# Weight buffers, staging tiles, score banks and the end of layer A regrouped in a two-layer attention trunk

## The chip, the cores and the metric

One core of one Trainium2 chip runs the whole program. The metric is device time in microseconds of one execution, the median of three runs. An execution that is profiled gives, besides its time, a span (first to last instruction) and the instructions of each engine.

## What is computed

A trunk of two layers over 528 positions (16 learned meta tokens, then 512 frames), 1024 wide, in float32, and a last norm; the meta rows are dropped from the output. Attention is block-causal: a query sees keys of its own chunk of 64 frames and of earlier ones; the 16 meta tokens are a chunk of their own that everybody sees.

```python
# layer A: differential attention, 8 heads of 2 x 64, values of 128
q, k, v = split(rms_norm(h) @ w_qkv); q, k = rotary(q), rotary(k)
a = softmax(q1 @ k1.T) - lam * softmax(q2 @ k2.T)
h = h + (rms_norm(a @ v) * (1 - lam_init)) @ w_o
h = h + (silu(conv3(rms_norm(h) @ w_a)) * (rms_norm(h) @ w_b)) @ w_out      # 2816 wide
# layer B: latent attention, 16 heads, keys of 64 + 32 rotary, values of 64
c_q = rms_norm(rms_norm(h) @ w_dq); q = c_q @ w_uq
c_kv, k_rope = split(rms_norm(h) @ w_dkv); k, v = split(rms_norm(c_kv) @ w_ukv)
h = h + softmax(q @ [k, k_rope].T) @ v @ w_o
h = h + conv_ffn(h)
out = rms_norm(h)[16:]
```

## The kernel before, in words

**Layout.** Activations lie transposed: 128 partitions of features, positions along the free dimension, in 8 feature tiles. Every float32 operand of a large product is split into a high part (a cast to the fast float32 format) and a low part (the difference), and a product is three: high x high, low x high, high x low (`mm3`, L163 to L166).

**Weights.** `wload` (L120) fetches weights over SP's queue into a raw tile (`rawtile`, L117: 1024 columns, 2 slots), and `wsplit` (L104) makes pairs of 512 columns: ScalarE casts the high part (L109), VectorE, or GpSimd while the attention runs, subtracts for the low part (L110). There are 6 slots for pairs (`WBUF`). An output tile of 8 input tiles of 128 columns takes two pairs. The second product of a feed-forward block in layer A has 22 input tiles, so 6 pairs for one output tile. `wload2` fetches two neighbouring output tiles at once, 256 columns. In the last product of the kernel (L1357) the weights are the moving side, a row of 128 inputs is two pairs, and the last `NL` = 3 rows are held together while the four query tiles are finished one after the other.

**Attention scores.** `scores` (L380) makes, for one head and one of its softmaxes, four query tiles that see 144, 272, 400 and 528 keys. It is cut into three steps, s0, s1 and s2. s0 makes the 144 and the 528, the latter as 256 and 272 in two separate banks; s1 the 400 and, beside them, the scores of the 16 meta queries, which it takes from a product with all 128 query columns; s2 the 272. For each, VectorE masks a corner (L393) and reduces to the negative maximum (L394), and ScalarE does the exponential and its row sum (L397). The two halves of the 528 have two maxima, two exponentials and two sums, which L410 and L428 join. All four tiles rotate through `NS` = 3 PSUM banks; two more (psD) serve the projections and three (psT) the transposes and values.

**The order** of each engine's instructions is worked out when the program is built: a planner goes through the program with its own cost estimates and starts on each engine what is ready, earlier statements first (and those under `soon` earlier than they stand). On the chip each engine then runs its list in that order and waits by semaphores. SP issues nearly all DMAs from one queue. So a later statement fills TensorE's holes where its operands are there.

**The end of layer A.** For each of 8 heads: projection of the next head (`qkproj`), scores, `vproj`, the two softmaxes joined (L600), transposes, values, and later `finish_a`, which norms finished heads and writes them as `oh`, `ol`. The root of the norm is done on GpSimd (`soft`), so that ScalarE's table for the exponential stays loaded; for the last head it is ScalarE's square root, which needs another table. To have that loaded early, a dummy square root (L588) reads one sum of the last score set. The meta rows have their own small attention (`meta_soft_a`, `meta_a`); those of the last 8 - KA = 3 heads come at the very end. `out_proj` is two products: heads 0 to KA - 1 (KA = 5) for all 8 output tiles, which can run as filler while later heads are not finished, then heads KA to 7 added to it. In each, one output tile is two halves of 264 positions, and each half adds up its input tiles in one bank of psD.

**Layer B** runs 16 heads in the same manner. `to_heads` (L1022) takes a projected pair of heads from PSUM, splits it into a staging tile `st` (2 slots) and sends the two heads to their own tiles by two DMAs (L1029), since they must change partitions; the queues for weights and for these transfers are the same one. The planner's filler here is a list with due times (`add`, `fill`).

## Time and profile before

| | |
|---|---|
| median of three runs | 1312.9 us (1310.15 to 1313.72) |
| the profiled execution's own time | 1312.65 us |
| its span | 1310.8 us |
| TensorE marked busy | 1279.3 us, 98% of the span |
| VectorE, ScalarE, GpSimd busy | 62%, 47%, 16% |
| mean granted TensorE clock | 0.992 |

Layer A's attention takes the first 300 us, its feed-forward block runs to 690, layer B's latents and attention to about 937, and the second feed-forward block and the final norm to the end. TensorE's matmuls are pipelined and their ends are modelled, so the start of one to the start of the next is the better measure of what one costs. In a row of the timeline the bracket at the end says how long the engine had been idle before it and what ended that.

### The profile page before, as it was taken

The numbers are of one execution on the slowest core, as the hardware profiler recorded it, in microseconds if no ns is written. First come the engines' busy times: TensorE is split into PE (matmuls) and PEld (weight loads), VectorE is DVE, ScalarE is ACT, GpSimd is POOL, SyncE is SP. The second block draws the span as 40 slices with busy tenths as digits, with TensorE's granted clock in tenths as the row PEclk, the third lists the DMA queues.
The fourth block names the chain that finished last, engine by engine and source line by source line (L and its number), as shares of the span: only waits on it lengthen the run. The fifth ranks groups of instructions, "written<-read, shape, count | busy, mean of one in ns | idle before, by whom it ended". The sixth has DMA issues, their size and how long they took to land.

```text
span 1310.8 us, 23833 instructions
## 1 busy us (share of the span) xinstructions
PE 1279.3 (98%) x9412; PEld 1212.6 (93%) x9412; DVE 814.4 (62%) x1702; ACT 619.9 (47%) x1319; POOL 206.1 (16%) x249
## 2 busy tenths in 40 slices
PE   9999999989999999999999899999999999999997
PEld 9899989989999999999999889999899999998886
DVE  6768887667666666533345778885866666662224
ACT  6666566555333433322234677874543333342223
POOL 5333541120000000000021644432200000000000
PEclk9999999989999999999999999999999999999999
DMA  6211211123233332333333545412332333332222
GB/s 211 82 54 56 71 53 49 57 73 100 82 97 90 88 97 82 92 89 90 89 109 62 120 101 122 116 43 81 98 96 87 92 97 97 96 100 92 87 93 81
DMA packets 166000, 117.13 MB, mean 89 GB/s; under 512 B 21248, under 2 KB 154688, under 8 KB 165888
## 3 DMA queue, kind: packets, MB, share of 16 engines
q1 hardware_dynamic: 165888, 115.61, 30.9%
q8 instruction: 74, 1.21, 0.4%
q14 instruction: 38, 0.31, 0.1%
HBM read 102.21 MB, written 2.10 MB: 80 GB/s over the span
## 4 chain that ended last, share of the span: by engine, by line
PE 76%; DVE 3%; ACT 2%; DMA 2%; POOL 1%; issue 1%; SPq 0%; ACTq 0%; POOLq 0%; DVEq 0%
PE psd L166 58%; PE psd L1357 9%; PE b L389 2%; PE ovb L1124 1%; PE tp L1091 1%; PE psd L1061 1%; DVE wlo L110 1%; DMA kt<-st 1%; PE ov L630 1%; DMA q<-st 0%; DVE nm L394 0%; PE tpm L1113 0%; ACT e L397 0%; ACT whi L109 0%; DVE xl L277 0%
## 5 line engine op out<-in xcount | busy, mean ns | idle before, releaser
L166 PE MATMUL psd<-xh,whi 128*128 128x264 f32 (+3 forms) x1664 | 494.2, 297 | 3.1 <-DVE qk L524 2.1
L166 PE MATMUL psd<-xh,wlo 128*128 128x264 f32 (+3 forms) x1664 | 493.1, 296 | 0.0
L166 PE MATMUL psd<-xl,whi 128*128 128x264 f32 (+3 forms) x1664 | 492.2, 296 | 0.7 <-DVE xl L349 0.5
L109 ACT CAST whi<-raw 128x512 fp32r<-128x512 f32 (+2 forms) x346 | 199.7, 589 | 378.7 <-PE psd L166 341.4
L166 PEld LDWEIGHTS psd<-xh,whi 128*128 128x128 f32 x1664 | 313.5, 189 | 12.3 <-DVE qk L524 2.8
L166 PEld LDWEIGHTS psd<-xl,whi 128*128 128x128 f32 x1664 | 313.5, 188 | 9.7 <-DVE xl L349 0.9
L166 PEld LDWEIGHTS psd<-xh,wlo 128*128 128x128 f32 x1664 | 313.4, 188 | 8.2 <-issue 0.4
L110 DVE TENSOR_TENSOR wlo<-raw,whi 128x512 fp32r<-128x512 f32 (+1 forms) x265 | 180.4, 686 | 129.2 <-ACT whi L109 128.0
L110 POOL TENSOR_TENSOR wlo<-raw,whi 128x512 fp32r<-128x512 f32 (+2 forms) x81 | 101.2, 1262 | 135.1 <-ACT whi L109 127.6
L166 PE MATMUL psd<-gh,whi 128*128 128x264 f32 x352 | 100.1, 285 | 0.0
L166 PE MATMUL psd<-gl,whi 128*128 128x264 f32 x352 | 99.9, 284 | 0.0
L166 PE MATMUL psd<-gh,wlo 128*128 128x264 f32 x352 | 99.8, 283 | 0.0
L397 ACT ACTIVATE e<-b,nm 128x272 f32<-128x272 f32 (+3 forms) x160 | 76.5, 481 | 33.5 <-DVE nm L394 19.2
L103 DVE TENSOR_TENSOR wlo<-raw,whi 128x512 fp32r<-128x512 f32 x44 | 28.7, 689 | 86.2 <-ACT whi L102 86.2
L131 POOL TENSOR_TENSOR raw<-raw,smalls 128x1024 f32<-128x1024 f32 x5 | 10.1, 2012 | 384.3 <-DVE acc L251 369.2
L260 DVE TENSOR_TENSOR hT<-psd,hT 128x264 f32<-128x264 f32 (+1 forms) x80 | 33.6, 424 | 57.7 <-PE psd L166 57.6
L102 ACT CAST whi<-raw 128x512 fp32r<-128x512 f32 x44 | 25.4, 619 | 92.7 <-PE psd L1357 75.9
L166 PEld LDWEIGHTS psd<-gl,whi 128*128 128x128 f32 x352 | 66.3, 188 | 0.0
L166 PEld LDWEIGHTS psd<-gh,wlo 128*128 128x128 f32 x352 | 66.3, 188 | 0.0
L166 PEld LDWEIGHTS psd<-gh,whi 128*128 128x128 f32 x352 | 66.2, 188 | 0.0
L394 DVE TENSOR_REDUCE nm<-b 128x1 f32<-128x272 f32 (+3 forms) x160 | 63.7, 423 | 1.2
L761 DVE TENSOR_TENSOR apad<-psd,rt 128x264 f32<-128x264 f32 (+1 forms) x88 | 37.5, 429 | 41.6 <-PE psd L166 41.6
(340 smaller groups left out, 2385.5 us busy)
## 6 DMA issues: line engine op xcount, KB each, us to landing
raw<-in_ffn_w_in SPq DMA_DIRECT2D x88, 512.0 KB
raw<-in_ffn_w_out SPq DMA_DIRECT2D x38, 512.0 KB
raw<-in_w_qkv SPq DMA_DIRECT2D x21, 512.0 KB
q<-st SPq DMA_DIRECT2D x28, 132.0 KB
kt<-st SPq DMA_DIRECT2D x28, 132.0 KB
raw<-in_ffn_w_out SPq DMA_DIRECT2D x8, 384.0 KB
hT<-in_h SPq DMA_DIRECT2D x8, 264.0 KB
q<-y SPq DMA_DIRECT2D x32, 66.0 KB
```

The source lines that it names most:

```text
L102: act.copy(hi, src)
L103: dve.tensor_tensor(lo, src, hi, ALU.subtract)
L109: act.copy(hi, src)
L110: wlo_engine[0].tensor_tensor(lo, src, hi, ALU.subtract)
L166: pe.matmul(ps[:rows, :n], a, xx[:, t0:t0 + n], start=first and ci == 0, stop=last and ci == 2)
L260: dve.tensor_tensor(hT[:, m, a:a + w], ps[:, :w], hT[:, m, a:a + w], ALU.add)
L389: pe.matmul(ps, q[:, q0:q0 + P], k[:, k0:k0 + n], start=i == 0, stop=i == len(parts) - 1)
L394: dve.tensor_reduce(nm[:, c:c + 1], ps, AX.X, ALU.max, negate=True)
L397: act.activation(e[:, o:o + ps.shape[1]], ps, AF.Exp, bias=nm[:, j:j + 1], accum_out=su[:, c:c + 1])
L630: pe.matmul(ov[:, j, :], ts[j][:, b * P:(b + 1) * P], vs[:, b, :], start=b == 0, stop=False)
L761: dve.tensor_tensor(a[:, off:off + n], ps[:, :n], rt[:, t0:t0 + n], ALU.mult)
L1357: pe.matmul(pso[t][n], a, ws[n][b], start=k == 0 and ci == 0, stop=k == NF - 1 and ci == 2)
```

## The change

Raw tiles go from 2 to 3 slots and split pairs from 6 to 5. A score set's 528 query tile is put into one tile of two neighbouring PSUM banks, of which there is one, reduced once and exponentiated once; the other two tiles of a set share one bank. The product for the meta scores loads 16 query columns in place of 128. Layer A's first out-projection part takes six heads, and the late meta rows are those of two heads, done ahead of the last head's transposes; the dummy square root stands behind the meta softmax and reads all four sums. Staging tiles in layer B go from 2 to 3 slots and lie in another pool.

```diff
-KA = KB = 5
+KA, KB = 6, 5
-WT, WBUF, LEAD = 512, 6, 2
+WT, WBUF, RBUF, LEAD = 512, 5, 3, 2
...
-        return wp.tile([P, 1024], F32, tag="raw", name="raw", bufs=2)[:, :n]
+        return wp.tile([P, 1024], F32, tag="raw", name="raw", bufs=RBUF)[:, :n]
...
-    first_ps = [[takeD() for _ in range(2)], [psS.tile([P, 512], F32, tag="s", name="psk") for _ in range(2)]]
+    psk = psS.tile([P, 1024], F32, tag="s2", name="psk", bufs=1)
+    first_ps = [[takeD() for _ in range(2)], [psk[:, i * 512:(i + 1) * 512] for i in range(2)]]
...
-        def qk(ps, q0, k0, n):
+        def qk(ps, q0, k0, n, nq=P):
             for i, (q, k) in enumerate(parts):
-                pe.matmul(ps, q[:, q0:q0 + P], k[:, k0:k0 + n], start=i == 0, stop=i == len(parts) - 1)
+                pe.matmul(ps, q[:, q0:q0 + nq], k[:, k0:k0 + n], start=i == 0, stop=i == len(parts) - 1)
...
-        bank = lambda n: psS.tile([P, 512], F32, tag="s", name=n)
+        bank = lambda n: psS.tile([P, 512], F32, tag="s", name=n, bufs=NS - 2)
 
         def s0():
-            b0 = bank("b0")
+
+            b0 = psS.tile([P, 1024], F32, tag="s2", name="b0", bufs=1)
             qk(b0[:, 0:256], 16, 0, 256)
             qk(b0[:, 256:512], 400, 0, 256)
+            qk(b0[:, 512:784], 400, 256, 272)
             negmax(b0[:, 0:144], 0, 80)
-            negmax(b0[:, 256:512], 3)
-            b1 = bank("b1")
-            qk(b1[:, 0:272], 400, 256, 272)
-            negmax(b1[:, 0:272], 4, 208)
-            dve.tensor_tensor(nm[:, 3:4], nm[:, 3:4], nm[:, 4:5], ALU.min)
+            negmax(b0[:, 256:784], 3, 464)
             ex(b0[:, 0:144], J0[0], 0, 0)
-            ex(b0[:, 256:512], J0[3], 3, 3)
-            ex(b1[:, 0:272], J0[3] + 256, 3, 4)
+            ex(b0[:, 256:784], J0[3], 3, 3)
...
-            qk(b2[:, 400:416], 0, 0, NM)
+            qk(b2[:NM, 400:416], 0, 0, NM, NM)
...
-            dve.tensor_tensor(su[:, 3:4], su[:, 3:4], su[:, 4:5], ALU.add)
...
         if h == HA - 1:
-
-            act.activation(s1a[:, 0, 0:1], es[1][1][:, 3:4], AF.Sqrt)
             ms = meta_soft_a(KA, 8 - KA)
+
+            act.activation(s1a[:, 0, :], es[1][1][:, 0:4], AF.Sqrt)
...
             dve.scalar_tensor_tensor(e1[:, sl], e2[:, sl], cc[:, j:j + 1], e1[:, sl], ALU.mult, ALU.add)
+        if h == HA - 1:
+
+            meta_a(KA, 8 - KA, *ms, soft=False)
...
         osb_s[h] = osb
-        if h == HA - 1:
-            meta_a(KA, 8 - KA, *ms, soft=False)
...
         if h == 5:
-            finish_a(4, KA)
+            finish_a(4, 5)
             meta_a(4, KA - 4, *meta_soft_a(4, KA - 4))
         if h == 6:
-            finish_a(KA, 7)
+            finish_a(5, 7)
...
-            st = ab0.tile([P, 2, HL], F32R, tag="st", name="st", bufs=2)
+            st = ab.tile([P, 2, HL], F32R, tag="st", name="st", bufs=3)
```

The one other line gives a PSUM tile of the first norm the same slot count as the score bank.

## Rows read from the trace of the kernel before

**Rows 1.** The page, busy time by engine.
```profile
PE 1279.3 (98%) x9412; PEld 1212.6 (93%) x9412; DVE 814.4 (62%) x1702; ACT 619.9 (47%) x1319; POOL 206.1 (16%) x249
```
**Rows 2.** The chain that ended last: start, us, what.
```profile
303.60 387.03 PE psd L166 x3185
```
**Rows 3.** Windows: length, busy PE, PEld, DVE, ACT, POOL, granted clock, DMA share, GB/s.
```profile
60.00:70.00 10.00, 9.75 (x68) 9.48 (x69) 5.32 (x23) 5.46 (x17) 0.52 (x1) 0.83 0.16 54
...
270.00:280.00 10.00, 8.47 (x50) 8.21 (x51) 4.72 (x11) 3.36 (x7) 0.00 (x0) 0.69 0.18 52
...
330.00:340.00 10.00, 10.00 (x84) 10.00 (x84) 6.00 (x11) 3.45 (x6) 0.00 (x0) 1.00 0.36 106
...
780.00:790.00 10.00, 8.37 (x61) 8.06 (x60) 8.40 (x23) 7.84 (x24) 6.88 (x9) 0.91 0.58 145
790.00:800.00 10.00, 9.93 (x71) 9.25 (x71) 6.80 (x21) 7.05 (x21) 4.37 (x6) 0.91 0.57 123
```
**Rows 4.** Timeline of layer A's end: ScalarE's table loads, then VectorE, then TensorE.
```profile
243.34 1.28 ACT L588 ACT_TABLE_LOAD   x1
...
245.34 1.28 ACT L397 ACT_TABLE_LOAD   x1
...
267.71 1.28 ACT L645 ACT_TABLE_LOAD   x1
...
243.08 0.73 DVE L670 SCALAR_TENSOR_TENSOR ol<-po,gsub,oh 128x512 fp32r<-128x512 f32 x1
...
247.86 0.69 DVE L110 TENSOR_TENSOR wlo<-raw,whi 128x512 fp32r<-128x512 f32 x1 [2.08 <-ACT whi L109]
...
250.38 0.39 PE L166 MATMUL psd<-oh,whi 128*128 128x264 f32 x1 [2.13 <-DVE hT L260]
...
271.28 0.50 PE L465 MATMUL psv<-ident,om 16*128 16x16 f32 x3 [3.75 <-DVE om L703]
```
**Rows 5.** Groups by form, TensorE, 221 to 243.8 us.
```profile
L166 PE MATMUL psd<-oh,whi 128*128 128x264 f32 x39 | 11.3, 290 | 0.0
```
**Rows 6.** Timeline of TensorE: short products in layer A, in layer B, with 16-column weights.
```profile
38.18 0.17 PE L389 MATMUL b<-ks,qs 128*128 128x16 f32 x1
...
38.52 0.28 PE L166 MATMUL psd<-xl,whi 128*128 128x264 f32 x1
...
743.79 1.05 PE L389 MATMUL b<-kt,q 96*128 96x400 f32 x6
...
744.90 0.28 PE L1061 MATMUL psd<-whi,ckl 128*128 128x256 f32 x1
...
833.23 1.06 PE L458 MATMUL psd<-vms,emT 16*16 16x64 f32 x16
```
**Rows 7.** Waits of ScalarE, 715 to 880 us: us in total, times, longest.
```profile
ACT st L102 <- DMA q<-st: 4.4, 7, 1.0
```
**Rows 8.** Waits of TensorE, 715 to 880 us, the same columns.
```profile
PE psd L166 <- DVE st L103: 1.6, 1, 1.6
PE b L389 <- DMA kt<-st: 1.4, 1, 1.4
```
**Rows 9.** Groups by form, whole run, VectorE and ScalarE: scores.
```profile
L410 DVE TENSOR_TENSOR nm<-nm 128x1 f32<-128x1 f32 x32 | 10.9, 342 | 0.3
...
L397 ACT ACTIVATE e<-b,nm 128x272 f32<-128x272 f32 x64 | 30.9, 483 | 8.5 <-DVE nm L394 8.3
L397 ACT ACTIVATE e<-b,nm 128x400 f32<-128x400 f32 x32 | 18.9, 592 | 4.0 <-DVE smeta L420 2.1 <-DVE nm L410 1.4 <-DVE su L428 0.3
```
**Rows 10.** Groups by form, whole run: weight splits and the last additions.
```profile
L109 ACT CAST whi<-raw 128x512 fp32r<-128x512 f32 x292 | 179.5, 620 | 365.5 <-PE psd L166 331.0 <-DMA raw<-in_ffn_w_out 9.3 <-issue 8.7
...
L110 DVE TENSOR_TENSOR wlo<-raw,whi 128x512 fp32r<-128x512 f32 x242 | 171.4, 711 | 127.9 <-ACT whi L109 126.8
...
L1373 DVE TENSOR_TENSOR htok<-psd,htok 128x512 f32<-128x512 f32 x8 | 5.4, 686 | 5.1 <-PE psd L1357 5.1
```
**Rows 11.** Timeline of TensorE, its last product.
```profile
1303.40 0.39 PE L1357 MATMUL psd<-whi,glb 128*128 128x512 f32 x1
```

More of the change, by code (lines that the diff above doesn't have):

```diff
@@ L482, in tile_trunk @@
     sp.dma_start(smalls, small[:, :NGAIN + 132])
-    some = iter([psT.tile([P, 512], F32, tag="t", name="psr"), psS.tile([P, 512], F32, tag="s", name="psr")])
+    some = iter([psT.tile([P, 512], F32, tag="t", name="psr"), psS.tile([P, 512], F32, tag="s", name="psr", bufs=NS - 2)])
     with tc.manual_schedule(engines={mybir.EngineType.PE}):
```

## The prediction, made before the changed kernel ran

> **What bounds the kernel.** I read the page first. TensorE is marked busy for 98% of the span [rows 1], so only two things can shorten the run: less TensorE work, or fewer of the holes in which it waits or runs at the lower clock. In layer A's feed-forward block a product of 264 columns starts every 387.03 / 3185 = 121.5 ns against 264 / 2.4 GHz = 110 ns [rows 2]: no hole there. The 10 us windows show where holes are [rows 3]: 330 to 340 is full; 60 to 70, 270 to 280, 780 to 790 and 790 to 800 have granted clocks of 0.83, 0.69, 0.91 and 0.91. A share below 1 is time at 1.2 instead of 2.4 GHz, and 10 x (1 - share) us of work are lost: 1.7, 3.1, 0.9 and 0.9 us. Each low stretch follows a hole. I then looked at who ends the holes, in layer A's last head [rows 4] and in layer B's first heads [rows 7, 8].
>
> The sum is made against the profiled execution's own 1312.65 us (span 1310.8); the median of the runs shown is 1312.9, so 0.25 above.
>
> **The end of layer A.** Before, ScalarE loads a table at 243.34 (square root, the early dummy), at 245.34 (back to the exponential, because a score tile and the meta softmax still need it) and at 267.71 (square root again), 1.28 us each [rows 4]. The first two hold up the next weight cast, VectorE idles 2.08 us for it with the evacuation of hT behind it, and TensorE waits 2.13 us for a bank at 250.38. The third lies on the last head's norm; TensorE has run out of out-projection work and waits 3.75 us at 271.28. The changed dummy reads all four sums, so it runs behind all exponentials, and it stands behind the meta softmax: one load is left, where nothing hurries. KA = 6 also puts 8 tiles x 2 halves x 3 = 48 products, 48 x 0.1215 = 5.8 us, ahead of the second wait, which outlasts 3.75. Both waits and the 3.1 us of low clock go: -9.0 us.
>
> The other side of KA = 6: no tile of the first part can finish before head 5's output, whose low half is written at 243.08 [rows 4]. Two banks of psD hold 5 of 6 steps each, 30 products, and then the first part stops. Before, it ran 39 + 39 + 38 = 116 in that stretch (three groups, of which one stands in [rows 5]): 86 products, 10.4 us, that filled TensorE between the scores and values of heads 6 and 7. Lower bound of the loss: nothing, if those chains move up into the freed places; upper: 10.4 plus 3.1 of low clock. The chains are bound half by TensorE's own queue and half by the softmax engines, so I take half, 5.2, plus 1.7 of low clock (as at 60 to 70). Net -9.0 + 6.9 = **-2.1 us** (ends -9.0 and +4.5). The calls of finish_a do the same as before, and meta_a(4, 2) has the instructions of meta_a(4, 1), on wider rows. Moving meta_a(6, 2) before the transposes passes neither SP's nor GpSimd's queue (it has no DMA, and its root is on ScalarE); it adds its few 16-row VectorE operations ahead of head 7's transposes; the first part's products then cover it, and if that cover were gone TensorE would wait there again, the 3.75 us of before at most.
>
> **Short meta scores.** In layer A two 16-column products and one of 264 take 38.52 - 38.18 = 0.34 us, so the two cost 0.22. In layer B three of 400 (178 ns each by the 11.5 ns over the column count), three of 16 and one of 256 (118 ns) take 744.90 - 743.79 = 1.11, so three cost 0.46 [rows 6]. The nearest row with a 16-column stationary side is 16 products in 1.06 us, 66 ns each [rows 6]. That would save 0.09 per set in A and 0.26 in B, x 16 each = 5.6 us. The next full weight load behind the short products stays uncovered, so I take **-3.2 us** (ends 0 and -5.6).
> By the Trainium skill, "TensorE: Matmul & The Clock Gate", section "LDWEIGHTS (loading the stationary operand)", a weight load takes the loaded columns / 1.2 ns, 107 against 13; the estimate by that page is 80 x 94 ns = 7.5 us and the sum 4.3 us lower. The row above is slower per product than that, and the sum keeps it.
>
> **Three staging tiles and three raw tiles.** ScalarE waits seven times, 4.4 us, for a staging tile that a DMA still reads; each wait stands in its queue ahead of exponentials [rows 7]. TensorE waits 1.6 us once for the evacuation through such a tile [rows 8], and the two windows at 0.91 around it lose 0.9 each [rows 3]. The third tile removes the slot wait; the third raw tile lets SP's queue pass weight loads that now wait for a slot in front of the staging transfers. I take 1.6 + 1.8 = **-3.4 us** (ends 0, and -4.8 with the 1.4 us wait on kt [rows 8]). Next late would be the landing of those transfers.
>
> **Scores in two banks.** Per set and of 32 sets it removes a minimum (0.34), an addition like it, one reduction's start and one exponential's start (272 columns take 0.48) [rows 9]. This is relief on VectorE and ScalarE, which TensorE rarely waits for: **-0.5 us** (ends 0 and -4). In return the last tile of a set waits for the exponential of the third where it waited for the first's, and with it all that stands behind it in TensorE's queue, transposes and projections; rival 3 prices it. psk only changes its bank.
>
> **Five split pairs.** In steady blocks a tile needs two pairs, and a split (0.62 + 0.71 us [rows 10]) fits many times into a tile's 5.8 us: nothing. Layer A's second feed-forward product needs six pairs per output tile (22 steps, 4 per pair): the sixth is split after the second half's first 12 products have freed one; the second half's other products cover it, so again nothing, and rival 2 is the case without cover. At the very end three rows need six pairs for all four query tiles at once. The sixth can be split only when the last query tile has used the first, so all four second halves end in the last 12 products, where before the ends were spread. Two more tiles than before then queue on VectorE behind the last product at 1303.40 [rows 11]: addition 0.69 each [rows 10], a product by the norm's gain about the same, a scaling. Ends 0 and 2 x 2.1; I take **+2.0 us**.
>
> Sum: -2.1 - 3.2 - 3.4 - 0.5 + 2.0 = -7.2, so 1305.45, forecast **1305.5 us**.
>
> **Rivals.** A difference under 0.3%, 3.9 us, can't be told from none here: faster is below 1309.0, slower above 1316.8.
> 1. Cover lost: the first part of the out-projection stands still until head 5 is done and nothing moves up. +4.5 in place of -2.1: 1312.0. For it: the 116 products. Against: VectorE and ScalarE are busy 62% and 47% of the span [rows 1], so the chains have room to move up.
> 2. Slower: five pairs are too few where one group needs six (8 tiles of layer A's second feed-forward product) or two neighbours need three each (3 boundaries in either out-projection): TensorE waits a whole split, 1.33 us, at 14 places, +18.6: 1324. It decides from nine such places. For it: ScalarE's casts already wait for TensorE to free a pair all along [rows 10]. Against: eight PSUM banks let other products go first.
> 3. One score bank in the ring: in each of layer B's 16 heads TensorE waits one exponential of 400 columns (0.59 [rows 9]): +9.4, 1315. Against: that exponential mostly follows the others within a microsecond before as well.
> The Trainium skill's same page, section "A second HAM failure mode: psum-queue depth-cycling", says that cycling through banks can make TensorE idle in small pieces until its clock swings; whether it does here hangs on those small waits.
> 4. The staging wait only becomes a wait for the transfer itself: -3.4 is not had, 1308.9.
>
> **Numbers.** Forecast 0.57; rival 1 0.13, rival 2 0.17, rival 3 0.07, rival 4 0.06. Faster is the forecast, 0.57. Same is rivals 1 and 4 and most of 3, 0.25 in all; slower is rival 2 and the worst of 3, 0.18. The range goes from 1296 (layer A's end at its best with the larger meta saving) to 1317, which takes in rivals 1, 3 and 4 and the cheaper half of rival 2.
>
> **What would show it.** Right: one table load between 240 and 275; no hole over 1 us before the last head's norm; holes between the scores of head 7 instead; the 16-column products under 0.1 us each; no ScalarE wait on the staging transfers; four additions behind the last product. Wrong: holes in the second feed-forward product or at the out-projections' tile boundaries, a low clock at 225 to 245, or a granted clock below 1 in more windows of layer B.

## The result and the profile after

The change makes the kernel slower: a median of 1336.07 us of four runs (1332.62 to 1337.39) against 1313.31 of four of the kernel before (1310.15 to 1317.1), a ratio over the runs of 1.0163 with a 95% interval from 1.0138 to 1.0188 (the quotient of the two medians is 1.0173). The forecast of 1305.5 and its whole range, to 1317, lie below. The profiled execution took 1332.62 us with a span of 1330.8, 20.0 above the span before. Four places in the trace say where they are: the start of layer A's feed-forward block (the last row-sum product of its norm, L215, 0.4 us ahead of the chain's piece in [rows 2]), the same place of layer B's feed-forward block, the last product, and the end.

| us | before | after | difference |
|---|---|---|---|
| layer A's attention, to its feed-forward block | 303.2 | 317.7 | +14.5 |
| from there to layer B's feed-forward block | 634.2 | 634.4 | +0.2 |
| from there to the last product | 366.0 | 366.0 | 0 |
| behind the last product | 7.4 | 12.7 | +5.3 |

The page's busy time and the long piece of the chain that ended last (start, us, what) answer [rows 1, 2]:

```profile
PE 1279.9 (96%) x9412; PEld 1208.1 (91%) x9412; DVE 811.6 (61%) x1602; ACT 608.9 (46%) x1249; POOL 203.3 (15%) x249
```
```profile
318.07 386.06 PE psd L166 x3177
```

TensorE has as many products and as much busy time as before, and layer A's feed-forward block runs at the same 121.5 ns per product. What was lost is in holes: TensorE's idle time, the span less the busy time, went from 31.5 to 50.9 us. (In the busy time two things about cancel: some 4 us less work for the meta scores, as a run below shows, and a mean granted clock of 0.988 in place of 0.992, an estimated 5 us.) The windows of the changed kernel (columns as in [rows 3]) show the worst of them:

```profile
190.00:200.00 10.00, 5.47 (x44) 4.80 (x42) 8.77 (x21) 6.14 (x12) 4.95 (x6) 1.00 0.17 40
200.00:210.00 10.00, 6.57 (x30) 5.63 (x30) 7.89 (x22) 3.36 (x11) 7.09 (x22) 0.52 0.01 2
...
270.00:280.00 10.00, 10.00 (x86) 9.90 (x87) 2.49 (x6) 2.79 (x6) 0.00 (x0) 1.00 0.17 54
780.00:790.00 10.00, 9.66 (x78) 9.24 (x76) 9.31 (x25) 6.39 (x18) 5.40 (x7) 1.00 0.47 102
```

From 190 to 200 TensorE is busy for 5.47 us, and in the next window the granted clock is 0.52: nearly all of it at 1.2 GHz. The same two windows before:

```profile
190.00:200.00 10.00, 9.69 (x81) 9.10 (x81) 8.12 (x11) 8.21 (x16) 8.57 (x14) 1.00 0.16 51
200.00:210.00 10.00, 10.00 (x82) 9.35 (x81) 7.79 (x27) 5.59 (x18) 0.00 (x0) 1.00 0.05 14
```

The places that the change was expected to mend, 270 to 280 and 780 to 790, are mended. TensorE's waits from 60 to 320 us (us in total, times, longest):

```profile
PE b L390 <- DVE qs L539: 6.6, 1, 6.6
PE p L609 <- DVE e L597: 5.3, 2, 4.7
PE psd L166 <- DVE qk L521: 3.2, 2, 3.0
PE b L390 <- ACT e L398: 2.4, 3, 1.2
```

All four stand in the loop over heads: scores wait for the next head's rotated queries, transposes for the joined softmax, and scores for an exponential, that is for their own bank. The timeline from 187 to 203 us, the second score set of head 5 (heads counted from 0), shows how the first comes about (rows of TensorE, ScalarE and VectorE):

```profile
187.34 0.45 PE L390 MATMUL b<-ks,qs 128*128 128x400 f32 x1
...
189.09 0.60 ACT L398 ACTIVATE e<-b,nm 128x400 f32<-128x400 f32 x1 [0.35 <-DVE smeta L418]
...
192.16 0.29 PE L390 MATMUL b<-ks,qs 128*128 128x272 f32 x1
...
192.65 0.11 DVE L394 MEMSET b<- 64x64 f32 x1 [0.42 <-PE b L390]
...
193.24 1.25 DVE L532 TENSOR_TENSOR sw<-sw,sr 80x1056 f32<-80x1056 f32 x1
...
197.51 1.26 DVE L697 SCALAR_TENSOR_TENSOR mv<-ms,mv 16x4 f32<-16x4 f32 x1
...
199.15 2.00 DVE L597 SCALAR_TENSOR_TENSOR e<-e,cc 128x144 f32<-128x144 f32 x4
...
201.18 0.70 DVE L539 SCALAR_TENSOR_TENSOR qs<-qk,qs 64x528 fp32r<-64x528 f32 x1
...
202.03 0.88 PE L390 MATMUL b<-ks,qs 128*128 128x256 f32 x2 [6.57 <-DVE qs L539]
```

The same set before, from 176 to 184 us:

```profile
179.92 0.34 PE L389 MATMUL b<-ks,qs 128*128 128x400 f32 x1
...
182.19 0.29 PE L389 MATMUL b<-ks,qs 128*128 128x272 f32 x1
...
182.30 0.59 ACT L397 ACTIVATE e<-b,nm 128x400 f32<-128x400 f32 x1 [0.30 <-DVE smeta L420]
```

Before, the 272 scores start 0.11 us ahead of the exponential of the 400: they have a bank of their own. After, both tiles share the one ring bank, so the 272 must follow that exponential, the planner has put other products ahead of them, and they start 4.82 us behind the 400 instead of 2.27. VectorE's mask of these scores comes that much later, and in VectorE's fixed order the rotation of the next head, the join and the low parts of the next queries stand behind it. By then TensorE has run through all that stands ahead of the next head's scores in its own order, and waits 6.57 us. VectorE works through nearly all of that hole (6.44 of 6.57 us): what costs is where the late scores stand in its order, not a wait of its own.

At the other end, the tail (timeline behind 1317 us):

```profile
1317.13 2.48 DVE L1371 TENSOR_TENSOR htok<-psd,htok 128x512 f32<-128x512 f32 x4 [2.12 <-PE psd L1355]
...
1318.10 0.40 PE L1355 MATMUL psd<-whi,glb 128*128 128x512 f32 x1
...
1322.64 4.98 SPq L1381 DMA_DIRECT2D out_dram<-htok  x8
...
1325.41 1.32 ACT L1378 ACTIVATE htok<-htok,fr 128x512 f32<-128x512 f32 x2
```

All eight output transfers are issued behind the last product; before, the first went out 2.7 us ahead of it, in this row of the timeline from 1296 us (the last product is [rows 11]):

```profile
1300.74 7.38 SPq L1383 DMA_DIRECT2D out_dram<-htok  x8
```

### The profile page after: what moved, and what is told of

It reads as the page before. It is cut to its first block, busy times and chain, and to the rows that moved or that the text cites. A ratio compares the mean times of both kernels' runs of the same rounds, so it can differ in the third digit from the quotient of the medians.

```text
span 1330.8 us, 23733 instructions
## 1 busy us (share of the span) xinstructions
PE 1279.9 (96%) x9412; PEld 1208.1 (91%) x9412; DVE 811.6 (61%) x1602; ACT 608.9 (46%) x1249; POOL 203.3 (15%) x249
## 4 chain that ended last, share of the span: by engine, by line
PE 83%; DVE 7%; ACT 3%; DMA 2%; POOL 2%; issue 1%; SPq 1%; ACTq 0%; DVEq 0%; POOLq 0%
PE psd L166 63%; PE psd L1355 9%; PE b L390 3%; PE ov L630 1%; DMA sw<-qkraw 1%; PE ovb L1122 1%; PE tp L1089 1%; PE psd L1059 1%; ACT e L398 1%; PE p L609 1%; DVE e L597 1%; DVE nm L395 1%; DVE osb L663 1%; DVE ptl L103 1%; DMA q<-st 0%
## 5 line engine op out<-in xcount | busy, mean ns | idle before, releaser
L110 POOL TENSOR_TENSOR wlo<-raw,whi 128x512 fp32r<-128x512 f32 (+2 forms) x81 | 97.4, 1213 | 174.9 <-ACT whi L109 169.4
L398 ACT ACTIVATE e<-b,nm 128x400 f32<-128x400 f32 (+3 forms) x128 | 68.4, 536 | 35.7 <-DVE smeta L418 15.9
L395 DVE TENSOR_REDUCE nm<-b 128x1 f32<-128x144 f32 (+3 forms) x128 | 62.7, 498 | 2.0
L1355 PE MATMUL psd<-wlo,ghb 128*128 128x512 f32 x176 | 58.4, 397 | 0.0
```

What stands on the lines that cost most here:

```text
L110: wlo_engine[0].tensor_tensor(lo, src, hi, ALU.subtract)
L395: dve.tensor_reduce(nm[:, c:c + 1], ps, AX.X, ALU.max, negate=True)
L398: act.activation(e[:, o:o + ps.shape[1]], ps, AF.Exp, bias=nm[:, j:j + 1], accum_out=su[:, c:c + 1])
L1355: pe.matmul(pso[t][n], a, ws[n][b], start=k == 0 and ci == 0, stop=k == NF - 1 and ci == 2)
```

## The experiments

Three theories were put to the runs. **Theory 1**: five split pairs are too few. **Theory 2**: a score ring of one bank beside the two-bank tile is too little. **Theory 3**: neither resource matters in itself; every edit makes the planner put the instructions into another order, and some orders cost layer A's attention several us. The table has all kernels: the ratio to the kernel before with its interval, taken over the runs of both (the quotient of the medians differs from it by up to 0.13%), then from the one profile of each the start of layer A's feed-forward block, the stretch from there to layer B's feed-forward block, the time behind the last product, and the mean time that a head's scores take in layer A (from the first to the last of each 24 score products, 192 in all; where heads overlap it is a little more than that). The feed-forward block of layer B took 366.0 us in every one. One profile is one run: the kernel with the staging edit alone has the same TensorE order as before through all of layer A and reads 1.7 us later, and in eight pairs of kernels that have the same TensorE order through layer A or through the middle, that stretch differs by up to 1.8 us. So differences under 2 us in the third and fourth columns say nothing. A profiled execution can also lie off its kernel's median: that of order_evictions was the longest of ten, 6.7 us above the median, so its 307.4 is too high by an unknown part of that; the others lie within 3.5 us.

| kernel | ratio | layer A | middle | tail | scores |
|---|---|---|---|---|---|
| before | 1 | 303.2 | 634.2 | 7.4 | 14.4 |
| after | 1.0163 (1.0138, 1.0188) | 317.7 | 634.4 | 12.7 | 19.6 |
| only_buffers | 1.0129 (1.0108, 1.0149) | 314.2 | 637.3 | 12.7 | 15.0 |
| only_banks | 1.0057 (1.0038, 1.0076) | 315.0 | 632.8 | 7.4 | 19.1 |
| only_end | 0.9997 (0.9985, 1.0010) | 303.6 | 637.3 | 7.4 | 14.3 |
| only_staging | 0.9987 (0.9973, 1.0001) | 304.9 | 634.6 | 7.4 | 14.4 |
| only_short_meta | 0.9941 (0.9926, 0.9956) | 300.8 | 630.8 | 7.4 | 13.3 |
| without_buffers | 1.0082 (1.0062, 1.0102) | 322.3 | 625.4 | 7.4 | 19.8 |
| without_banks | 1.0066 (1.0040, 1.0092) | 307.8 | 630.4 | 12.7 | 13.9 |
| five_pairs_only | 1.0154 (1.0127, 1.0182) | 313.0 | 639.1 | 13.0 | 15.1 |
| banks_without_merging | 1.0071 (1.0047, 1.0095) | 312.1 | 637.0 | 7.4 | 22.2 |
| order_weights | 1.0020 (1.0005, 1.0036) | 304.1 | 637.6 | 7.4 | 15.3 |
| order_evictions | 0.9992 (0.9972, 1.0012) | 307.4 | 636.0 | 7.4 | 14.6 |
| five_pairs_other_order | 1.0078 (1.0059, 1.0096) | 308.1 | 640.9 | 12.7 | 14.6 |
| banks_other_order | 1.0072 (1.0057, 1.0087) | 316.0 | 632.8 | 7.4 | 19.7 |
| change_splits_on_vector | 1.0108 (1.0089, 1.0128) | 312.6 | 634.5 | 12.7 | 22.2 |
| before_splits_on_vector | 0.9978 (0.9965, 0.9991) | 297.6 | 637.2 | 7.4 | 15.8 |
| splits_and_staging | 0.9914 (0.9899, 0.9928) | 298.8 | 629.8 | 7.4 | 15.9 |
| splits_staging_meta | 0.9963 (0.9946, 0.9979) | 304.5 | 627.9 | 7.4 | 17.6 |
| splits_staging_meta_end | 0.9985 (0.9971, 0.9999) | 308.0 | 630.4 | 7.4 | 16.7 |

### One part of the change at a time

**Only the buffers.**

```diff
-WT, WBUF, LEAD = 512, 6, 2
+WT, WBUF, RBUF, LEAD = 512, 5, 3, 2
-        return wp.tile([P, 1024], F32, tag="raw", name="raw", bufs=2)[:, :n]
+        return wp.tile([P, 1024], F32, tag="raw", name="raw", bufs=RBUF)[:, :n]
```

> The kernel before with three raw tiles and five split pairs, nothing else. The changed kernel loses 14.5 us in layer A's attention and 5.3 us behind the last product. Theory 1 (too few split pairs): both losses stand here, layer A 10 to 15 us longer and the end 5 us longer, 1328 to 1334. Theory 2 (the score banks): only the end is longer, 1315 to 1320. Theory 3 (no single part: each part moves the planner's order, and VectorE then meets GpSimd's weight splits at bad places): layer A anywhere from -5 to +8, the end +5.

1332.29 us: 11.0 in layer A, 3.1 in the middle and 5.3 behind the last product. The largest part of what the whole change loses comes with this edit alone, most of it in layer A's attention and not in the feed-forward products.

**Only the score banks**: the two-bank tile with its merged reduction and exponential, and one ring bank.

```diff
-        bank = lambda n: psS.tile([P, 512], F32, tag="s", name=n)
+        bank = lambda n: psS.tile([P, 512], F32, tag="s", name=n, bufs=NS - 2)
...
-            b0 = bank("b0")
+            b0 = psS.tile([P, 1024], F32, tag="s2", name="b0", bufs=1)
...
-            negmax(b0[:, 256:512], 3)
-            b1 = bank("b1")
...
+            negmax(b0[:, 256:784], 3, 464)
```

> The kernel before with the 528 query tile in two neighbouring banks, one reduction and one exponential for it, and one bank for the other two tiles of a set. Theory 1: 1308 to 1315, as VectorE and ScalarE have less to do. Theory 2: the third and fourth tile of a set wait for each other, layer A 10 to 15 us longer, 1322 to 1330, layer B within 3 us. Theory 3: layer A -5 to +8.

1322.5 us: layer A loses 11.8, the middle is 1.4 shorter, which is under the scatter. So two parts cost 11.0 and 11.8 us in layer A, each by itself, and 14.5 together: the losses don't add up.

**Only the end of layer A**, with the moved calls that the diff of the whole change shows:

```diff
-KA = KB = 5
+KA, KB = 6, 5
...
+            act.activation(s1a[:, 0, :], es[1][1][:, 0:4], AF.Sqrt)
```

> The kernel before with layer A's end rearranged alone (six heads in the first out-projection part, the late meta rows earlier, the dummy root behind the meta softmax). By the prediction 1302 to 1311 (-9.0 + 6.9, ends -9.0 and +4.5); by rival 1 of it 1316 to 1318. Theories 1 and 2 want nothing of layer A's first six heads to change; theory 3 lets those move by several us too.

1314.09 us, no difference. The waits of [rows 4] are gone, and instead layer A's last heads have holes. The windows of this kernel, columns as before:

```profile
230.00:240.00 10.00, 6.76 (x38) 6.19 (x37) 7.10 (x29) 5.39 (x16) 2.62 (x13) 0.80 0.00 1
240.00:250.00 10.00, 10.00 (x73) 9.74 (x72) 8.96 (x31) 6.25 (x16) 0.00 (x0) 0.86 0.07 21
```

3.2 us of TensorE and, by the granted clock, 3.4 us of work are lost there, and from 221 to 243.8 us the first out-projection part runs 48 products (three groups of 16) where it ran 116 [rows 5]. What the edit gives it takes back.

**Only the three staging tiles.**

```diff
-            st = ab0.tile([P, 2, HL], F32R, tag="st", name="st", bufs=2)
+            st = ab.tile([P, 2, HL], F32R, tag="st", name="st", bufs=3)
```

> The kernel before with three staging tiles in the other pool. By the prediction 1308 to 1312 (-3.4, ends 0 and -4.8), with no ScalarE wait on a staging transfer; by its rival 4 no change, 1312 to 1314. Layer A is the same in either: the edit lies behind it.

1312.51 us, a gain at the edge of what can be told. The waits from 715 to 885 us, first ScalarE's, then TensorE's, answer [rows 7, 8]:

```profile
ACT st L102 <- DMA q<-st: 3.3, 3, 2.4
...
ACT st L102 <- DMA kt<-st: 0.4, 1, 0.4
```
```profile
PE b L389 <- DMA q<-y: 2.9, 1, 2.9
...
PE psd L166 <- DVE st L103: 0.7, 1, 0.7
```

ScalarE's seven waits became four, of 3.7 in place of 4.4 us, and TensorE's wait for the evacuation fell from 1.6 to 0.7, but a wait of 2.9 us for a transfer of queries came in.

**Only the short meta scores.**

```diff
-            qk(b2[:, 400:416], 0, 0, NM)
+            qk(b2[:NM, 400:416], 0, 0, NM, NM)
```

> The kernel before with the short meta scores alone (16 query columns as the stationary side, 80 products). By the prediction's term 3.2 us less, 1310; if the full weight load behind the short product takes back what it saves, 1312 to 1314; under theory 3 a shift of 1 to 4 us either way in layer A besides, from the order.

1306.84 us beside 1314.68, the best part of the change. TensorE's timeline in layer A's first set:

```profile
38.78 0.17 PE L389 MATMUL b<-ks,qs 128*16 128x16 f32 x1
38.80 0.17 PE L389 MATMUL b<-kl,qs 128*16 128x16 f32 x1
38.83 0.37 PE L166 MATMUL psd<-xh,whi 128*128 128x264 f32 x1
39.03 0.28 PE L166 MATMUL psd<-xl,whi 128*128 128x264 f32 x1
```

The same place before has the short products' starts at 38.18 and 38.21, and the product behind them at

```profile
38.32 0.37 PE L166 MATMUL psd<-xh,whi 128*128 128x264 f32 x1
```

The two short products and the next now start within 0.05 us, where it was 0.14. The product behind them takes 0.20 us to the next start in place of its usual 0.12, but it did so before as well (38.32 to 38.52). Over all sets, from the first short product to the second product behind them less that product's own spacing, the median fell from 222 to 138 ns in layer A and from 334 to 171 in layer B: 16 x 84 + 16 x 163 = 4.0 us of TensorE's work. The span is 5.8 us shorter, and the rest is in holes that were smaller; why they were was not looked into.

### One part taken out of the change

**Six pairs and two raw tiles again**, the diff of the buffers turned round.

> The changed kernel with its six split pairs and two raw tiles back; all other parts of the change stay. Theory 1, the five pairs are to blame where they are used: layer A's attention comes back to about 304 us (as before, 303.2), the end behind the last product from 12.7 to 7.4 us, and the time is about 1317. Theory 2, the scores in two banks are to blame in layer A: only the 5.3 us at the end come back, layer A's feed-forward block still starts at about 315 to 317 us, and the time is 1328 to 1331. Theory 3, both parts only move instructions so that VectorE and GpSimd meet in the same place (the meta rows and norms behind head 4, 185 to 205 us): layer A keeps 8 to 14 us, as with the banks alone (11.8), and the time is 1322 to 1330; the hole stands between heads 3 and 5 again, whatever wait ends it.

1323.7 us. The end is back at 7.4, layer A is 4.6 us longer still, and the middle is 9.0 shorter. Theory 1 falls as the cause of layer A's loss: with six pairs and the new banks layer A is at its worst.

**Separate score banks again**, the diff of the banks turned round.

> The changed kernel with the scores of the last query tile in separate banks again, as before (three banks in the ring); all other parts stay. Theory 1 (five pairs): layer A still loses about 11 us as with the buffers alone, the end 5.3, so 1327 to 1333. Theory 2 (score banks): layer A comes back to about 304, the end keeps its 5.3 us, so about 1317 to 1319. Theory 3 (VectorE against GpSimd behind head 4): a loss of 8 to 14 us in layer A, the end's 5.3, about 1326 to 1332, with TensorE's longest holes at 185 to 205 us.

1321.07 us. Layer A is at 307.8, 9.9 us better than with the two-bank tile, and its longest hole stands elsewhere, from 233.8 us on (7.0 us, a transpose that waits for VectorE's scaling of the output).

### Whether it is the bank, the merging or the order

**Banks without merging**: the tile and the ring of the change, all reductions and exponentials as before.

```diff
-            b0 = bank("b0")
+            b0 = psS.tile([P, 1024], F32, tag="s2", name="b0", bufs=1)
...
-            b1 = bank("b1")
+            b1 = b0[:, 512:1024]
```

> The kernel before with the two-bank score tile and the single ring bank, but with the last query tile's reductions, exponentials, minimum and sum as they were (272 and 256 columns apart). Only the banks' use changes; VectorE and ScalarE keep all their work. Theory 2 (the ring's single bank is the cause): layer A still loses 8 to 14 us, and the sum is a few us above the banks with merging, 1323 to 1328, since the saved instructions are missing. If it is the merged, longer reductions and exponentials that hold the chains up, layer A loses under 4 us and the time is 1312 to 1317. Theory 3 gives no sign, only that layer A differs from the banks with merging by several us.

1323.17 us, layer A +8.9: the new use of the three banks is enough to cost it, and the merging is not what holds the chains up. Whether more of it comes from the one ring bank or from there being only one two-bank tile was not tried apart.

**Order alone.** Two numbers of the planner, in the kernel before, with all work and all buffers as they were.

```diff
-PRW, PRE = 400, 200
+PRW, PRE = 600, 200
```

> The kernel before with one number of the planner changed: the lead that weight loads get in its order, 600 for 400. No work, no tile and no buffer changes, and the first 402 TensorE instructions stand where they stood; of the 9213, 926 stand elsewhere. Theory 3 (the edits of the change cost layer A time by the order that they bring about, not by the resource that they take away): this order alone moves the start of layer A's feed-forward block by some us, 3 to 12 either way from 303.2, and the time by as much: 1300 to 1310 or 1317 to 1325. Theories 1 and 2 (a missing split pair or score bank is what TensorE waits for): nothing is missing here, so within 2 us of 303.2 and of 1313.

1316.72 us, layer A +0.9.

```diff
-PRW, PRE = 400, 200
+PRW, PRE = 400, 400
```

> The kernel before with another number of the planner changed: the lead of evictions, 400 for 200. Again no work, no tile and no buffer changes; 532 of the 9213 TensorE instructions stand elsewhere, the first of them at place 407. Theory 3: layer A's feed-forward block starts 2 to 10 us away from 303.2, on either side, and the time is outside 1309 to 1317. Theories 1 and 2: within 2 us of 303.2 and of 1313.

1312.07 us. Layer A reads +4.2, but in the one execution that lies 6.7 us above the median; the median is no longer than that of the kernel before. Both orders alone cost less than either part of the change, and the time hardly shows them. Theory 3 isn't shut out, but these two orders don't reach 11 us.

**Five pairs alone**, with the two raw tiles.

```diff
-WT, WBUF, LEAD = 512, 6, 2
+WT, WBUF, LEAD = 512, 5, 2
```

> The kernel before with five split pairs and its two raw tiles. Theory 1 (five pairs): layer A loses about 11 us as with both buffer edits, the end behind the last product goes from 7.4 to 12.7 us, and the time is 1329 to 1333. If the third raw tile was what cost layer A (weights loaded earlier, so splits in other places), layer A stays within 3 us of 303.2, only the end's 5.3 us come, and the time is 1317 to 1320. Theory 3: layer A is anywhere between 300 and 316, as the order falls out; the end costs 5.3 in any case.

1334.6 us: the third raw tile is not the cause, five pairs are, with 9.8 us in layer A, 4.9 in the middle and 5.6 at the end. TensorE's order in layer A is the same as with both buffer edits.

**The same resources under another order**: five pairs, and the banks of the change, each with the lead of evictions at 400.

```diff
-PRW, PRE = 400, 200
-WT, WBUF, LEAD = 512, 6, 2
+PRW, PRE = 400, 400
+WT, WBUF, LEAD = 512, 5, 2
```

> Five split pairs (two raw tiles) and the planner's lead of evictions at 400 instead of 200: five pairs under another order (972 of the 9213 TensorE instructions stand elsewhere than before, against 817 with five pairs alone). With six pairs that number moved the start of layer A's feed-forward block from 303.2 to 307.4 us. Theory 1, the missing pair costs layer A whatever the order: the block starts at 311 us or later, the end takes 12.7 to 13.0, and the time is 1330 to 1338. Theory 3, the order that five pairs happened to bring about is what costs: the block starts anywhere between 300 and 309, the end as before, and the time is 1317 to 1327.

> The scores in two banks (with merging) and the same number, 400 for 200: the single ring bank under another order (1571 TensorE instructions elsewhere than before). Theory 2, the single ring bank costs layer A whatever the order: its feed-forward block starts at 311 us or later, and the time is 1318 to 1328. Theory 3: anywhere between 300 and 309, and the time is 1305 to 1317.

This tells the two apart. With five pairs layer A is at 308.1, 0.7 us from six pairs in that same order. As the 307.4 of six pairs is too high, the ratios, which rest on every run, are the better witness. By them five pairs cost 1.54% in the first order and 0.86% in the other (1.0078 over 0.9992), some 20 and 11 us. The end and the middle take 10.5 and 10.2 of these, so some 10 and 1 us are left for layer A (an estimate). Most of the 9.8 us belonged to the particular order that five pairs brought about.

With the two-bank tile layer A is at 316.0, 8.6 from the same order without it. By the ratios the banks cost 0.57% and 0.80%, some 7.5 and 10.5 us, with the middle 1.4 and 3.2 shorter, so some 9 and 14 us in layer A (an estimate): the banks cost layer A in both orders that were tried. So theory 2 stands for layer A, and theory 1 for the end and, with the cause open, for the middle.

The last column shows what they do. In the ten kernels with three ring banks and GpSimd's splits a head's scores take 13.3 to 15.3 us, in the five with one ring bank and the same splits 19.1 to 22.2. That is 5.6 us more on average, some 45 us over eight heads, in which scores are under way; TensorE covers most of it with other products, but not the 9 to 19 us by which these five start the feed-forward block later than 303.2. TensorE's waits from 60 to 320 us say the same more directly: in all six kernels with one ring bank score products wait for an exponential, 2.4 to 6.4 us in total. With three ring banks ten of fourteen kernels have no such wait; one has 0.2 us and three, all with layer A's end or the short meta scores changed, have 3.2 to 9.1.

### VectorE beside GpSimd

In layer A the low parts of the weights are subtracted on GpSimd. These rows of the timeline of the changed kernel, GpSimd from 193 us on and VectorE beside it, show what that does:

```profile
194.69 4.07 POOL L110 TENSOR_TENSOR wlo<-raw,whi 128x512 fp32r<-128x512 f32 x2 [4.76 <-ACT whi L109]
...
196.34 1.25 DVE L682 TENSOR_TENSOR mt<-mt,smeta 16x32 f32<-16x32 f32 x1
```

and this is the 16 x 4 operation of L697 (in the timeline above) with the splits moved, from the groups by form:

```profile
L697 DVE SCALAR_TENSOR_TENSOR mv<-ms,mv 16x4 f32<-16x4 f32 x1 | 0.1, 121 | 0.0
```

0.12 us where it took 1.26. Beside the GpSimd subtractions this operation lasted until they ended: it ends at 198.77, the pair of subtractions at 198.76. It and that of L682, which lasts 0.16 us with the splits moved, make up some 2.2 of the 6.57 us for which TensorE waits at that place. Two runs move the splits, in the kernel before and in the changed one.

```diff
-    wlo_engine[0] = pool
+    wlo_engine[0] = dve
     nxt = qkproj(0)
```

> The changed kernel with one line more: in layer A the low parts of the weights are subtracted on VectorE and not on GpSimd (30 subtractions of 128x512, 43 us of GpSimd's time there, 0.7 us each on VectorE, so 21 us more on VectorE). Theory 3: small VectorE operations that now last 1.1 to 2.6 us beside a GpSimd subtraction fall to under 0.3, the holes at 185 to 205 us go, layer A's feed-forward block starts 6 to 14 us earlier, at 304 to 312, and the time is 1322 to 1330. Theories 1 and 2: five pairs and one ring bank stay what they are, VectorE has 21 us more to do, so layer A is no shorter or some us longer: 1336 to 1345.

> The kernel before with the same line: layer A's low parts on VectorE. It prices the line by itself. Theory 3 in its strict form (a meeting of the two engines costs wherever it happens): layer A's feed-forward block starts 0 to 6 us earlier than 303.2, and the time is 1307 to 1314. If VectorE's 21 us more lie on layer A's chains, it starts later by up to 10 us and the time is 1314 to 1323; then what the line gains in the changed kernel, less this, is the price of the meetings there.

1327.14 and 1310.11 us. Layer A gains 5.1 us in the one and 5.6 in the other, though VectorE has more to do, so the edit is worth some 5 us of layer A in both kernels; it changes the order too, so how much of this is the meetings is not shown. The change is not slower because of them: 297.6 against 312.6 is 15.0, and 303.2 against 317.7 is 14.5. The Trainium skill, "SBUF — State Buffer", section "Who interferes with whom", has this as a rule: the two engines share one pair of ports as an exclusive lock, not as a share of bandwidth. The rows agree in that the operation of L697 ended only when the subtraction did.

### A version that beats both

**Splits on VectorE and three staging tiles**, the two diffs above on the kernel before.

> A candidate: the kernel before with the three staging tiles and with layer A's low parts on VectorE, and nothing of the rest of the change. If the two gains add (0.13% and 0.22% alone), 1308 to 1310; if the staging gain was the scatter of two series of runs, 1310 to 1312; if the order that the two together bring about costs layer A or B something, 1312 to 1317.

1303.59 us beside 1314.68, 0.9914 of the kernel before: the best of all, and more than the two gains alone (0.22% and 0.13%). In layer A TensorE's order is that of the splits alone (298.8 against 297.6); what is more than the sum stands in the middle, 629.8, where the kernel before has 634.2, the splits alone 637.2 and the staging tiles alone 634.6. **With the short meta scores as well**, and **with layer A's end too**:

> A candidate: the kernel before with three staging tiles, layer A's low parts on VectorE, and the short meta scores; six split pairs, the ring of three score banks and layer A's end as before. If the short meta scores are less TensorE work and so keep their gain in any order (0.6% alone), the ratio is 0.984 to 0.988 and the time about 1295 to 1299. If part of it was the order of that one kernel, 0.988 to 0.992, 1299 to 1303.

> The same with layer A's end rearranged as in the change (KA = 6 and the three edits around it): everything of the change but the score banks and the buffers, with the low parts on VectorE. Alone the end was worth nothing (ratio 0.9997): if that holds here, within 2 us of the candidate without it. If the two holes at the end that it was made for stand in the candidate, they go, and it is 2 to 5 us shorter; if its order brings the low clock at 235 to 245 us of the end alone, 2 to 4 us longer.

1308.76 and 1313.17: both worse. The middle keeps the gain (627.9 against 629.8), and layer A loses 5.7. TensorE's timeline of the first of these kernels, from 180 to 193 us:

```profile
186.50 0.45 PE L389 MATMUL b<-ks,qs 128*128 128x400 f32 x1 [1.82 <-ACT e L397]
...
192.57 0.59 PE L389 MATMUL b<-ks,qs 128*128 128x272 f32 x1 [5.41 <-ACT e L397]
```

Two holes wait for an exponential to free a bank, both in head 6's first score set: less TensorE work, and an order in which three ring banks are too few as well. So theory 3 holds to this extent: the order that an edit brings about is worth some us by itself. It is some 9 us for five pairs, by the profiles (9.8 over six pairs in one order, 0.7 in the other) and by the ratios alike.

## Why the prediction was wrong

Two steps failed: the term for the score banks and the term for five split pairs. Between them they were put at +1.5 us; in layer A and at the end the whole change lost 14.5 and 5.3.

**The scores in two banks**: -0.5 us, ends 0 and -4, against +8.9 to +12.8 in layer A in the three kernels that have only this use of the banks (each against 303.2). The prediction called it relief on engines that TensorE rarely waits for, saw that the last tile would wait for the exponential of the third, and priced that in rival 3 as one exponential of 0.59 us in each head of layer B. Layer A's 16 score sets, which use the same banks, it left out without a reason. In layer B the banks cost nothing that can be told: the middle is 1.4 us shorter with the banks alone. The place is layer A. That the banks cost 9 to 14 us there is shown by taking them in and out; that the price is all that stands behind the late scores in VectorE's order, and not the exponential alone, is read from the one hole of 6.57 us, and the other holes were not followed like that. So rival 3 had the right wait, but neither its place nor its size. The Trainium skill, "TensorE: Matmul & The Clock Gate", section "A second HAM failure mode: psum-queue depth-cycling", has many small pauses between bursts make the clock swing. That isn't what the trace shows: the low clock, 0.52 from 200 to 210 us, follows one hole of 6.57 us, and in layer B, where TensorE waits for the exponential twice, 1.4 us in all, the window from 780 to 790 has 1.00.

**Five split pairs**: +2.0 with ends 0 and 4.2, against 20 us in the run with five pairs alone. All of the +2.0 was taken for the end, where the runs show 5.3 to 5.6 in all six kernels that have them. The term's count was short: it had two more tiles at an addition, a product and a scaling each. Behind the last product before stand one addition and one product by the gain; after, four additions in a row start 1 us ahead of it, and from then on seven products by the gain and, on ScalarE, seven squares follow in turns, so that the first output leaves 4.5 us after the last product. "In steady blocks nothing" held for layer A's feed-forward block: 386.06 against 387.03 us, and rival 2, which has its 14 places there and at the out-projections, is refuted: the changed kernel has no wait of TensorE for a split (`whi`, `wlo`) in the whole list of its waits. "Nothing" did not hold for layer A's attention, which the prediction didn't look at: 9.8 us in the order of the run with five pairs alone, though some 1 us in another; nor for the middle, 3.1 to 9.0 us in four pairs of kernels with and without (one of them with the third raw tile in it, one with both that and the rest of the change). There TensorE waits for the first queries' transfer, here after and before (waits, 715 to 885 us):

```profile
PE b L390 <- DMA q<-y: 3.1, 1, 3.1
```
```profile
PE b L389 <- DMA q<-y: 1.0, 1, 1.0
```

This wait is 2.9 us with six pairs and three staging tiles too, so why the middle is longer with five pairs stays open.

**The end of layer A.** -2.1, as -9.0 and +6.9; alone +0.4 in layer A and a ratio of 0.9997. Both halves came as described: one table load, in the changed kernel at 256.44 us, of [rows 4]'s two waits 0.9 us left, and holes in the last heads instead. Net a little worse, within the ends. In the -9.0 the low clock of 3.1 us was counted in full beside the wait of 3.75, though TensorE still waited in the first 1.3 us of that window; by the rows some 0.6 us stand in it twice.

**Short meta scores.** -3.2 taken, ends 0 and -5.6; TensorE's work fell by 4.0 us. The reason given for taking less than the end (the full weight load behind stays uncovered) is not what the trace shows: the 0.08 us on the product behind stand in layer A's rows before as well as after, so nothing is taken back there, and the 0.084 us saved per set is close to the 0.09 of the end. In layer B it is 0.16 of 0.26; there the 0.46 us before was read off one place, and the median over the sets is 0.33. By the Trainium skill, "TensorE: Matmul & The Clock Gate", section "LDWEIGHTS (loading the stationary operand)", the estimate was 7.5; the trace doesn't agree. The loads are recorded at 0.10 us for 16 columns and 0.19 for 128, and the short products, 70 and 83 ns each before (139 for two in layer A, 250 for three in layer B, to the next product's start), take 27.

**Three staging tiles.** -3.4 taken; the ratio alone gives -0.1%, 1.7 us, with 0 inside the interval. As rival 4 had it, a part of the wait became one for the transfer. In the changed kernel ScalarE still waits 3.9 us in three places for a staging transfer; the prediction had none left. (Rival 4's 1308.9 lies below the prediction's own bound for faster, 1309.0, and was counted as no difference.)

The sum was made term by term, as if each part acted where it was written. Nearly all of what was lost came from places that no edit names, above all from layer A's attention, where TensorE, VectorE and ScalarE run fixed orders against each other. The runs showed that there the sum of the parts isn't the whole: 11.0 and 11.8 made 14.5, and two gains of 0.2% and 0.1% made 0.9%.

## What to carry to other kernels

When a PSUM bank or a buffer is taken from a ring, look in every stage that uses the ring at what stands behind the late tile in each engine's order, not only at the one instruction that it now waits for. In a kernel whose order is planned at build time, an edit to any part of a tight stage changes the order of all of it; measure each part alone and together, run a change of order alone beside them as a yardstick, look at the medians beside a single profile, and don't add up gains. Before counting on GpSimd as a free helper, look for tiny VectorE operations that last as long as GpSimd's.

## What the runs showed of the hardware that was not expected

A VectorE operation of 16 x 4 elements lasted 1.26 us beside a GpSimd subtraction and 0.12 without, and the pair of subtractions beside it 4.07 us where one takes 1.5 us on average before (28 in 43.1 us, from 60 to 290 us). One hole of 6.57 us was followed by a window of 10 us at 0.52 of the full clock, which lost some 4 us more (10 x (1 - 0.52) = 4.8, less what fell into the hole's own last 2 us). A reduction over two neighbouring PSUM banks runs as one instruction: 528 columns in 698 ns, where 256 and 272 took 409 and 430.
